# Order of the last output blocks and the last LayerNorm of a two-layer decoder trunk

## The chip, the core and the metric

One core of a Trainium2 chip runs the whole program. The metric is device time in microseconds (us) from the start to the end of one execution; before the change the median of three runs is 1009.05 us. The engines named below are the tensor engine (PE, whose weight loads have a row of their own, PEld), the vector engine (DVE), the scalar engine (ACT), GpSimd (POOL) and the sync engine (SP), which here only issues transfers. ACT and POOL issue transfers too.

## The reference, cut to what matters

The trunk has two layers on 256 tokens of width 2048: a Mamba-2 layer and a sliding-window attention layer. Each ends in a residual sum and a LayerNorm. The change touches the very last part: the output projection of the attention layer, the residual sum and the last LayerNorm.

```python
def _layernorm(x, g, b):
    xf = x.astype(jnp.float32)
    mu = jnp.mean(xf, axis=-1, keepdims=True)
    var = jnp.mean(jnp.square(xf - mu), axis=-1, keepdims=True)
    y = (xf - mu) * lax.rsqrt(var + EPS) * g.astype(jnp.float32) + b.astype(jnp.float32)
    return y.astype(x.dtype)
...
    o = o * jax.nn.silu(gate)
    return o @ w_out
...
        x = _layernorm(ALPHA * x + h, ln_g[layer], ln_b[layer])
    return x
```

## The kernel before, in words

**Tiles.** The 256 tokens are two halves, h = 0 and h = 1, of 128 tokens each, one token to a partition. The residual stream is the tile `xr`, 128 partitions x 2 halves x 2048. The 2048 output columns are four blocks nb (c in the norm) of 512.

**Weights.** A unit is 128 x 2048 weights. It comes in two 512 KB transfers into `wr` (line 131, SP's queue) and is split into a rounded part `wh` (ACT, line 140) and the remainder `wl` (DVE, line 141). `next_unit()` hands out the next unit and loads two ahead.

**One output block** is `out_unit` (line 278): for one half and one block, 12 matmuls of 128x128 by 128x512 (lines 284 to 286: high by high, low by high, high by low, for four slices of the contraction) into one of four PSUM buffers `mm`; then DVE adds the sum to `xr` (line 293). After each block `norm_stats` (line 752) takes mean and variance of it on DVE.

**The end** is `out_last` (line 295), called for the last quarter of the contraction, whose four units hold all blocks nb = 0 to 3. Its order before: half 0 block 0, half 1 block 0, then half 0 blocks 1 to 3, then `done2(0)`, then half 1 blocks 1, 2 and 3 (block 3 as two blocks of 256 columns), then `done2(1)`.

**`done2(0)`**, the norm of half 0: `norm_scale` merges the statistics on DVE (line 756) and takes the reciprocal root by Ln and Exp on ACT (lines 758, 759). For each of four blocks: DVE makes t = (xr - mean) * g (line 1094), ACT scales t (line 1097), POOL adds b (line 1098), SP sends the block out (line 1099). This runs beside the matmuls of half 1.

**`done2(1)`**, the norm of half 1: nothing but this is left to do. PE puts b into three PSUM tiles `ax` (identity times b, line 1068; blocks 0 and 1 whole and half of block 2). ACT makes a diagonal `dg` of the scale (line 1069), DVE makes t for all four blocks (line 1074), PE adds `dg` times t (line 1080), ACT copies the sums to `xr` (line 1081) and sends them (line 1082). The other half of block 2 and block 3 are finished on DVE (line 1085) and sent by SP (line 1088).

**Order.** Each engine runs its instructions in the order in which the program was recorded (with some movement by the recording layer, which `keep_in_program_order` forbids for the instruction that it is given); engines wait for each other by semaphores. The buffers `t` (tag `pt`) are four.

Of the kernel before, what the change touches and what calls it, by code (L numbers as in the profile page):

```python
# [8 lines left out]
F32 = mybir.dt.float32  # L9
# [3 lines left out]
AF = mybir.ActivationFunctionType  # L13
ALU = mybir.AluOpType
AX = mybir.AxisListType

P = 128
# [48 lines left out]
def trunk(ctx: ExitStack, tc: tile.TileContext, A: dict, out: bass.AP, dbg=None):  # L66
    nc = tc.nc
    PSUM = bass.MemoryType.PSUM

    def pool(name, bufs=1, side=None, space=None, stack=ctx):  # L70
        kw = {"space": space} if space is not None else {}
        return stack.enter_context(
            tc.tile_pool(name=name, bufs=bufs, side=side, reuse_waits="tile", **kw)
        )
# [9 lines left out]
    def nm(s):  # L84
        uid[0] += 1
        return f"{s}_{uid[0]}"

    def mm_tile():
        return mm_ps.tile([P, 512], F32, tag="mm", name=nm("mm"), bufs=4)

    def ax_tile():
        return ax_ps.tile([P, 512], F32, tag="ax", name=nm("ax"), bufs=4)

    cc = cst.tile([P, 896], F32, tag="cc", name="cc")
    ident = cc[:, 0:128]
# [117 lines left out]
    def next_unit():  # L213
        load_next(min(used[0] + 1 + AHEAD, len(srcs)) - len(units))
        used[0] += 1
        return units[used[0] - 1]
# [29 lines left out]
    xr = xp.tile([P, 2 * D + 120], F32, tag="xr", name="xr")[:, : 2 * D].rearrange("p (h d) -> p h d", h=2)  # L246
# [27 lines left out]
    def pinned(m, pin):  # L274
        if pin:
            tc.keep_in_program_order(m)

    def out_unit(aH, aL, h, u, nb, first, rms=None, pin=False, c0=0, c1=512):

        ps = mm_tile()[:, : c1 - c0]  # L280
        hs = slice(h * P, (h + 1) * P)
        for k in range(4):
            ks = slice(k * 512 + c0, k * 512 + c1)
            pinned(nc.tensor.matmul(ps, aH[:, k, hs], u.h[:, ks], start=k == 0, stop=False), pin)  # L284
            pinned(nc.tensor.matmul(ps, aL[:, k, hs], u.h[:, ks], start=False, stop=False), pin)  # L285
            pinned(nc.tensor.matmul(ps, aH[:, k, hs], u.l[:, ks], start=False, stop=k == 3), pin)  # L286
        v = xr[:, h, nb * 512 + c0 : nb * 512 + c1]
        if first:
            nc.vector.scalar_tensor_tensor(v, v, ALPHA, ps, ALU.mult, ALU.add)
        elif rms is not None:  # L290
            nc.vector.scalar_tensor_tensor(v, ps, rms[:, h : h + 1], v, ALU.mult, ALU.add)  # L291
        else:
            nc.vector.tensor_tensor(v, v, ps, ALU.add)

    def out_last(aH, aL, stats, done):

        us = []
        for nb in range(4):
            us.append(next_unit())
            out_unit(aH, aL, 0, us[nb], nb, False)  # L300
            stats(0, nb)
            if nb == 0:
                out_unit(aH, aL, 1, us[nb], nb, False)
                stats(1, nb)
        done(0)
        for nb in range(1, 4):

            n = 256 if nb == 3 else 512
            for c0 in range(0, 512, n):
                out_unit(aH, aL, 1, us[nb], nb, False, None, False, c0, c0 + n)  # L310
                stats(1, nb, c0, c0 + n)
        done(1)

    def narrow(ps, u, k0, k1, pin=False):
        for k in range(k0, k1):
# [387 lines left out]
    for g in range(NG):  # L703
        t = 10 * g
# [44 lines left out]
    x1L = x1s.tile([P, KT, S], F32R, tag="x1L", name="x1L")  # L749

    def norm_stats(st, h, nb, c0=0, c1=512):
        nc.vector.bn_stats(st[:, h, nb + (c0 > 0), :], xr[:, h, nb * 512 + c0 : nb * 512 + c1])

    def norm_scale(lp, st, h, n=4):
        mv = lp.tile([P, 2], F32, tag="mv", name=nm("mv"), bufs=2)
        nc.vector.bn_aggr(mv[:], st[:, h, :n, :])
        rs = lp.tile([P, 1], F32, tag="rs", name=nm("rs"), bufs=2)
        nc.scalar.activation(rs[:], mv[:, 1:2], AF.Ln, bias=eps_t[:])
        nc.scalar.activation(rs[:], rs[:], AF.Exp, scale=-0.5)
        return mv, rs  # L760
# [42 lines left out]
    us = {}  # L803
    yHL, rms = gs[NG - 1].y, gs[NG - 1].rms
    for h, nb in ((0, 0), (1, 0), (0, 1), (0, 2), (0, 3), (1, 1), (1, 2), (1, 3)):
        if h == 0:
            us[nb] = next_unit()
        out_unit(*yHL, h, us[nb], nb, False, rms, True)
        norm_stats(st1, h, nb)
        if nb == 3:  # L810
            center(h)
        for c in {(1, 2): (0, 1), (1, 3): (2, 3)}.get((h, nb), ()):
            turn_x1(0, c, x1p, "x1", 2)
# [4 lines left out]
    bp = pool("bp")  # L818
# [36 lines left out]
    for h in range(2):  # L855
        ps = mm_tile()
# [43 lines left out]
    os_ = {}  # L900
# [153 lines left out]
    gp = pool("gp", side="right")  # L1054
    gb2 = [gp.tile([P, D], F32, tag=f"gb{i}", name=f"gb2_{i}") for i in range(2)]
    nc.gpsimd.dma_start(gb2[0][:], A["lng"][1].partition_broadcast(P))
    nc.gpsimd.dma_start(gb2[1][:], A["lnb"][1].partition_broadcast(P))
    st2 = bp.tile([P, 2, 5, 6], F32, tag="st", name="st2")

    def done2(h):  # L1060
        mv, rs = norm_scale(bp, st2, h, 4 + h)
        if h:

            dg = bp.tile([P, P], F32, tag="dg", name="dg")
            ends = (512, 512, 256, 0)
            pss = [ax_tile()[:, :n] for n in ends[:3]]
            for c, ps in enumerate(pss):
                nc.tensor.matmul(ps, ident, gb2[1][:, c * 512 : c * 512 + ends[c]], start=True, stop=False)
            nc.scalar.activation(dg[:], ident, AF.Copy, scale=rs[:])
            ts = []  # L1070
            for c in range(4):
                sl = slice(c * 512, (c + 1) * 512)
                t = bp.tile([P, 512], F32, tag="pt", name=nm("t"), bufs=4)
                nc.vector.scalar_tensor_tensor(
                    t[:], xr[:, h, sl], mv[:, 0:1], gb2[0][:, sl], ALU.subtract, ALU.mult
                )
                ts.append(t)
                if ends[c]:
                    sl = slice(c * 512, c * 512 + ends[c])
                    nc.tensor.matmul(pss[c], dg[:], t[:, : ends[c]], start=False, stop=True)  # L1080
                    nc.scalar.copy(xr[:, h, sl], pss[c])
                    nc.scalar.dma_start(out[h * P : (h + 1) * P, sl], xr[:, h, sl])
            for c in (3, 2):
                sl = slice(c * 512 + ends[c], (c + 1) * 512)
                nc.vector.scalar_tensor_tensor(
                    xr[:, h, sl], ts[c][:, ends[c] :], rs[:], gb2[1][:, sl], ALU.mult, ALU.add
                )
                nc.sync.dma_start(out[h * P : (h + 1) * P, sl], xr[:, h, sl])
            return
        for c in range(4):  # L1090
            sl = slice(c * 512, (c + 1) * 512)
            v = xr[:, h, sl]
            t = bp.tile([P, 512], F32, tag="pt", name=nm("t"), bufs=4)
            nc.vector.scalar_tensor_tensor(
                t[:], v, mv[:, 0:1], gb2[0][:, sl], ALU.subtract, ALU.mult
            )
            nc.scalar.activation(t[:], t[:], AF.Copy, scale=rs[:])
            nc.gpsimd.tensor_tensor(v, t[:], gb2[1][:, sl], ALU.add)
            nc.sync.dma_start(out[h * P : (h + 1) * P, sl], v)

    if PRE:
        tc.keep_in_program_order(nc.scalar.preload_act_table_set("natural_log_exp_and_others"))
    out_last(*os_[3], lambda *a: norm_stats(st2, *a), done2)


def _layout(inputs):
# [88 lines left out]
```

## Time and profile before

| | us |
|---|---|
| median of three runs | 1009.05 (1008.87 to 1010.24) |
| the profiled execution: its own time | 1009.92 |
| its span, first to last instruction | 1008.0 |
| last matmul of `out_unit` starts | 997.25 |
| last transfer is issued | 1003.65 |

The profile gives times in us from the start of the span. A row of the time-ordered view reads: start, duration, engine, line, operation, what is written from what, shapes, the count of instructions that were merged into the row, and in brackets the idle time of the engine before it and what ended it. A "q" behind an engine (SPq, ACTq) is its sequencer, where transfers are issued. Matmuls are pipelined: a row's duration is longer than the distance to the next one. A float32 matmul of 512 columns shows as two records.

### The profile page before, as it was taken

The page shows a single profiled execution, that of the slowest core. Times are in us where ns is not written, and L with a number is a line of the kernel's source. Part 1 is how long each engine was busy: PE and PEld are TensorE (multiplying, and loading weights), DVE is VectorE, ACT ScalarE, POOL GpSimd, SP SyncE. Part 2 cuts the span into 40 slices and gives each one's busy share as a digit, 9 for nine tenths or more (in the row PEclk, how much of TensorE's full clock was granted, in tenths as well). Part 3 has the DMA queues.
Part 4 walks back from the last instruction along what each step waited for, and adds up shares of the span by engine and source line. Part 5 has one row for each costly group of instructions (what it writes and reads, how often), then busy time and mean ns, then how long its engine had stood idle before and what let it go on. Part 6 is the DMA issues. An engine that isn't in the chain of part 4 may idle for free.

```text
span 1008.0 us, 17712 instructions
## 1 busy us (share of the span) xinstructions
PE 995.8 (99%) x7027; PEld 901.7 (89%) x7027; DVE 770.5 (76%) x1133; ACT 566.6 (56%) x947; POOL 103.5 (10%) x126
## 2 busy tenths in 40 slices
PE   8999999999999999999999999999999999999997
PEld 7999989999998998999999999888988878878975
DVE  5778977877786887686787687898688775775686
ACT  5576856647655654664654664566545543543642
POOL 0000403004003002100300300403000000000002
PEclk9999999999999999999999999999999999999999
DMA  8797576565666766656656556557754545545532
GB/s 316 264 290 251 207 249 195 173 238 164 216 211 187 228 197 201 202 191 201 206 175 224 154 187 221 168 160 246 232 196 140 185 149 180 174 147 178 173 129 84
DMA packets 58386, 198.80 MB, mean 197 GB/s; under 512 B 6496, under 2 KB 11008, under 8 KB 58048
## 3 DMA queue, kind: packets, MB, share of 16 engines
q1 hardware_dynamic: 55216, 188.20, 57.5%
q0 software_dynamic: 2336, 8.69, 2.7%
q8 instruction: 55, 0.90, 0.4%
q10 hardware_dynamic: 752, 0.79, 0.2%
q14 instruction: 27, 0.22, 0.1%
HBM read 195.43 MB, written 2.23 MB: 196 GB/s over the span
## 4 chain that ended last, share of the span: by engine, by line
PE 85%; DVE 6%; ACT 4%; DMA 3%; issue 2%; SPq 0%; ACTq 0%; DVEq 0%
PE mm L220 43%; PE mm L284 8%; PE mm L285 8%; PE mm L286 8%; PE mm L846 3%; PE mm L847 3%; PE mm L848 3%; DVE wl L141 2%; PE ax L564 2%; DMA wr<-in_wa 2%; PE ax L956 1%; PE ax L1014 1%; DVE cv L431 1%; ACT wh L140 1%; ACT e L484 1%
## 5 line engine op out<-in xcount | busy, mean ns | idle before, releaser
L141 DVE TENSOR_TENSOR wl<-wr,wh 128x1024 fp32r<-128x1024 f32 (+2 forms) x342 | 398.5, 1183 | 116.9 <-ACT wh L140 115.5
L140 ACT ACTIVATE wh<-wr 128x1024 fp32r<-128x1024 f32 (+2 forms) x342 | 337.8, 1011 | 218.9 <-PE mm L220 79.2
L220 PE MATMUL mm<-xH,wh 128*128 128x256 f32 x1280 | 356.5, 279 | 0.0
L220 PE MATMUL mm<-xL,wh 128*128 128x256 f32 x1280 | 355.5, 278 | 0.0
L220 PE MATMUL mm<-xH,wl 128*128 128x256 f32 x1280 | 355.2, 278 | 0.0
L220 PEld LDWEIGHTS mm<-xH,wh 128*128 128x128 f32 x1280 | 241.2, 188 | 2.2 <-ACT wh L173 0.7
L220 PEld LDWEIGHTS mm<-xL,wh 128*128 128x128 f32 x1280 | 241.2, 188 | 1.0
L220 PEld LDWEIGHTS mm<-xH,wl 128*128 128x128 f32 x1280 | 241.2, 188 | 0.0
L284 PE MATMUL mm<-wh,yH 128*128 128x512 f32 x256 | 101.5, 396 | 0.3 <-DVE xr L291 0.3
L285 PE MATMUL mm<-wh,yL 128*128 128x512 f32 x256 | 99.8, 390 | 0.0
L286 PE MATMUL mm<-wl,yH 128*128 128x512 f32 x256 | 99.7, 390 | 0.0
L580 POOL TENSOR_TENSOR yz<-yz,z 128x256 f32<-128x256 f32 x32 | 32.7, 1031 | 478.0 <-DVE yz L575 478.0
L431 DVE SCALAR_TENSOR_TENSOR cv<-mm,pc,cv 128x255 f32<-128x255 f32 x144 | 68.8, 478 | 5.3 <-ACT cv L429 4.0
L220 PE MATMUL mm<-x1H,wh 128*128 128x256 f32 x256 | 71.9, 281 | 0.0
L220 PE MATMUL mm<-x1H,wl 128*128 128x256 f32 x256 | 71.0, 277 | 0.0
L220 PE MATMUL mm<-x1L,wh 128*128 128x256 f32 x256 | 71.0, 277 | 0.0
L846 PE MATMUL mm<-wh,x1H 128*128 128x512 f32 x160 | 63.2, 395 | 0.0
L847 PE MATMUL mm<-wh,x1L 128*128 128x512 f32 x160 | 62.5, 391 | 0.2 <-DVE x1L L799 0.2
L848 PE MATMUL mm<-wl,x1H 128*128 128x512 f32 x160 | 62.4, 390 | 0.0
L284 PEld LDWEIGHTS mm<-wh,yH 128*128 128x128 f32 x256 | 48.1, 188 | 11.0 <-DVE z L517 1.0
L291 DVE SCALAR_TENSOR_TENSOR xr<-mm,r,xr 128x512 f32<-128x512 f32 x64 | 47.0, 745 | 13.4 <-PE mm L286 8.8
L286 PEld LDWEIGHTS mm<-wl,yH 128*128 128x128 f32 x256 | 48.1, 188 | 10.2
(192 smaller groups left out, 1331.8 us busy)
## 6 DMA issues: line engine op xcount, KB each, us to landing
wr<-in_wa SPq DMA_DIRECT2D x158, 512.0 KB, 4.9
wr<-in_wo SPq DMA_DIRECT2D x64, 512.0 KB, 4.2
wr<-in_wq SPq DMA_DIRECT2D x32, 512.0 KB, 4.5
wr<-in_wg SPq DMA_DIRECT2D x32, 512.0 KB, 4.7
wr<-in_wb SPq DMA_DIRECT2D x32, 512.0 KB, 4.6
rb<-rscr SPq DMA_DIRECT2D x11, 512.0 KB, 5.0
wr<-in_wkv SPq DMA_DIRECT2D x8, 512.0 KB, 4.5
el<-rscr SPq DMA_DIRECT2D x14, 256.0 KB, 4.7
```

The costliest lines, as they stand in the source:

```text
L140: nc.scalar.activation(h[:, sl], v, AF.Copy)
L141: m = nc.vector.tensor_tensor(l[:, sl], v, h[:, sl].bitcast(F32), ALU.subtract)
L220: m = nc.tensor.matmul(ps, a, b, start=first and i == 0, stop=last and i == 2)
L284: pinned(nc.tensor.matmul(ps, aH[:, k, hs], u.h[:, ks], start=k == 0, stop=False), pin)
L285: pinned(nc.tensor.matmul(ps, aL[:, k, hs], u.h[:, ks], start=False, stop=False), pin)
L286: pinned(nc.tensor.matmul(ps, aH[:, k, hs], u.l[:, ks], start=False, stop=k == 3), pin)
L291: nc.vector.scalar_tensor_tensor(v, ps, rms[:, h : h + 1], v, ALU.mult, ALU.add)
L431: nc.vector.scalar_tensor_tensor(a[:, sft:], ps[:, : S - sft], w(3 - sft), a[:, sft:], ALU.mult, ALU.add)
L580: nc.gpsimd.tensor_tensor(v, v, st.z[i][:], ALU.mult)
L846: pinned(nc.tensor.matmul(ps[:], x1H[:, kk, hs], u.h[:, ks], start=kk == 0, stop=False), pin)
L847: pinned(nc.tensor.matmul(ps[:], x1L[:, kk, hs], u.h[:, ks], start=False, stop=False), pin)
L848: pinned(nc.tensor.matmul(ps[:], x1H[:, kk, hs], u.l[:, ks], start=False, stop=kk == KT - 1), pin)
```

## The change

`out_last` now takes all four blocks of half 0 first, then all four of half 1 (block 3 in two again). The norm of half 0 is in two parts: blocks 0 and 1 are handed to DVE, ACT and POOL right after half 0's statistics, block 2 after half 1's block 0, block 3 after half 1's block 1. For half 1's blocks 0 and 1, DVE makes xg = xr * g as soon as the block is there, without the mean.

The norm of half 1 uses two diagonals for blocks 0 and 1: `dg[0]` holds the scale, `dg[1]` the scale times the negative mean (`nmean`, on DVE). PE sums identity times b, `dg[0]` times xg and `dg[1]` times g. Blocks 3 and 2 are done wholly on DVE, each by two instructions. The transfers out are then issued in the order 3, 0, 2 from SP, and 1 from ACT. Nearly all instructions of this end are pinned to the order written.

```diff
-    def out_last(aH, aL, stats, done):
+    def out_last(aH, aL, stats, first_done, product, last_done):
...
         for nb in range(4):
             us.append(next_unit())
             out_unit(aH, aL, 0, us[nb], nb, False)
             stats(0, nb)
-            if nb == 0:
-                out_unit(aH, aL, 1, us[nb], nb, False)
-                stats(1, nb)
-        done(0)
-        for nb in range(1, 4):
+        rest = first_done()
+        for nb in range(4):
 
             n = 256 if nb == 3 else 512
             for c0 in range(0, 512, n):
                 out_unit(aH, aL, 1, us[nb], nb, False, None, False, c0, c0 + n)
                 stats(1, nb, c0, c0 + n)
-        done(1)
+            if nb < 2:
+                product(nb)
+                rest(2 + nb)
+        last_done()
...
+    xg = gp.tile([P, 2, 512], F32, tag="xg", name="xg")
...
+    def product2(nb):
+        sl = slice(nb * 512, (nb + 1) * 512)
+        ordered(nc.vector.tensor_tensor(xg[:, nb, :], xr[:, 1, sl], gb2[0][:, sl], ALU.mult))
+
+    def first_done2():
+        mv, rs = norm_scale(bp, st2, 0, 4)
+
+        def piece(c):
...
+            ordered(
+                nc.vector.scalar_tensor_tensor(t[:], v, mv[:, 0:1], gb2[0][:, sl], ALU.subtract, ALU.mult)
             )
             nc.scalar.activation(t[:], t[:], AF.Copy, scale=rs[:])
             nc.gpsimd.tensor_tensor(v, t[:], gb2[1][:, sl], ALU.add)
+            nc.sync.dma_start(out[0:P, sl], v)
+
+        piece(0)
+        piece(1)
+        return piece
+
+    def last_done2():
+
+        pss = [ax_tile() for _ in range(2)]
+        for c, ps in enumerate(pss):
+            nc.tensor.matmul(ps, ident, gb2[1][:, c * 512 : c * 512 + 512], start=True, stop=False)
+        mv, rs = norm_scale(bp, st2, 1, 5)
+        nmean = bp.tile([P, 1], F32, tag="nmean", name="nmean")
+        ordered(nc.vector.tensor_scalar(nmean[:], mv[:, 0:1], -1.0, None, ALU.mult))
+        dg = bp.tile([P, 2, P], F32, tag="dg", name="dg")
+        ordered(nc.scalar.activation(dg[:, 0, :], ident, AF.Copy, scale=rs[:]))
+        ordered(nc.scalar.activation(dg[:, 1, :], dg[:, 0, :], AF.Copy, scale=nmean[:]))
+        for c, ps in enumerate(pss):
+            ordered(nc.tensor.matmul(ps, dg[:, 0, :], xg[:, c, :], start=False, stop=False))
+            sl = slice(c * 512, (c + 1) * 512)
+            ordered(nc.tensor.matmul(ps, dg[:, 1, :], gb2[0][:, sl], start=False, stop=True))
+            ordered(nc.scalar.copy(xr[:, 1, sl], ps))
+        for c in (3, 2):
...
+            ordered(nc.vector.scalar_tensor_tensor(
+                t[:], xr[:, 1, sl], mv[:, 0:1], gb2[0][:, sl], ALU.subtract, ALU.mult
+            ))
+            ordered(nc.vector.scalar_tensor_tensor(
+                xr[:, 1, sl], t[:], rs[:], gb2[1][:, sl], ALU.mult, ALU.add
+            ))
+        for c, eng in ((3, nc.sync), (0, nc.sync), (2, nc.sync), (1, nc.scalar)):
+            sl = slice(c * 512, (c + 1) * 512)
+            ordered(eng.dma_start(out[P : 2 * P, sl], xr[:, 1, sl]))
...
-    out_last(*os_[3], lambda *a: norm_stats(st2, *a), done2)
+    out_last(*os_[3], stats2, first_done2, product2, last_done2)
```

More of the change, by code (lines that the diff above doesn't have):

```diff
@@ L751, in norm_stats @@
     def norm_stats(st, h, nb, c0=0, c1=512):
-        nc.vector.bn_stats(st[:, h, nb + (c0 > 0), :], xr[:, h, nb * 512 + c0 : nb * 512 + c1])
+        return nc.vector.bn_stats(st[:, h, nb + (c0 > 0), :], xr[:, h, nb * 512 + c0 : nb * 512 + c1])
     def norm_scale(lp, st, h, n=4):
@@ L1058, in trunk @@
     st2 = bp.tile([P, 2, 5, 6], F32, tag="st", name="st2")
[L1060 to L1090, printed above, removed]
@@ L1091, in done2, with stats2 @@
+    xg = gp.tile([P, 2, 512], F32, tag="xg", name="xg")
+    ordered = tc.keep_in_program_order
+    def stats2(h, nb, c0=0, c1=512):
+        ordered(norm_stats(st2, h, nb, c0, c1))
+    def product2(nb):
[4 more added lines that the diff above has]
+        def piece(c):
             sl = slice(c * 512, (c + 1) * 512)
-            v = xr[:, h, sl]
+            v = xr[:, 0, sl]
@@ L1093, in done2 @@
             t = bp.tile([P, 512], F32, tag="pt", name=nm("t"), bufs=4)
-            nc.vector.scalar_tensor_tensor(
-                t[:], v, mv[:, 0:1], gb2[0][:, sl], ALU.subtract, ALU.mult
+            ordered(
+                nc.vector.scalar_tensor_tensor(t[:], v, mv[:, 0:1], gb2[0][:, sl], ALU.subtract, ALU.mult)
             )
@@ L1098, in done2 @@
             nc.gpsimd.tensor_tensor(v, t[:], gb2[1][:, sl], ALU.add)
-            nc.sync.dma_start(out[h * P : (h + 1) * P, sl], v)
+            nc.sync.dma_start(out[0:P, sl], v)
[19 more added lines that the diff above has]
+            sl = slice(c * 512, (c + 1) * 512)
+            t = bp.tile([P, 512], F32, tag="pt", name=nm("t"), bufs=4)
+            ordered(nc.vector.scalar_tensor_tensor(
[5 more added lines that the diff above has]
+        for c, eng in ((3, nc.sync), (0, nc.sync), (2, nc.sync), (1, nc.scalar)):
+            sl = slice(c * 512, (c + 1) * 512)
+            ordered(eng.dma_start(out[P : 2 * P, sl], xr[:, 1, sl]))
     if PRE:
         tc.keep_in_program_order(nc.scalar.preload_act_table_set("natural_log_exp_and_others"))
-    out_last(*os_[3], lambda *a: norm_stats(st2, *a), done2)
+    out_last(*os_[3], stats2, first_done2, product2, last_done2)
 def _layout(inputs):
```

## The prediction

> **What bounds the kernel now.** I read the page first, then the chain of waits, then the time-ordered view of the last 35 us, engine by engine.
>
> ```profile
> span 1008.0 us, 17712 instructions
> ...
> PE 995.8 (99%) x7027; PEld 901.7 (89%) x7027; DVE 770.5 (76%) x1133; ACT 566.6 (56%) x947; POOL 103.5 (10%) x126
> ...
> PE 85%; DVE 6%; ACT 4%; DMA 3%; issue 2%; SPq 0%; ACTq 0%; DVEq 0%
> ```
>
> PE bounds the whole, and the change takes no matmul of the projection away. What can move is the tail, in which the chain leaves PE. Here is DVE in it:
>
> ```profile
> 976.58 2.36 DVE L141 TENSOR_TENSOR wl<-wr,wh 128x1024 fp32r<-128x1024 f32 x2 [0.23 <-ACT wh L140]
> ...
> 986.54 0.69 DVE L293 TENSOR_TENSOR xr<-xr,mm 128x512 f32<-128x512 f32 x1 [1.30 <-PE mm L286]
> 987.26 0.69 DVE L752 BATCH_NORM_STATS2 st<-xr 128x6 f32<-128x512 f32 x1
> 989.26 0.69 DVE L293 TENSOR_TENSOR xr<-xr,mm 128x512 f32<-128x512 f32 x1 [1.30 <-PE mm L286]
> 989.99 0.69 DVE L752 BATCH_NORM_STATS2 st<-xr 128x6 f32<-128x512 f32 x1
> 990.71 0.26 DVE L756 BATCH_NORM_AGGREGATE mv<-st 128x2 f32<-128x24 f32 x1
> 991.01 3.78 DVE L1094 SCALAR_TENSOR_TENSOR t<-xr,mv,gb 128x512 f32<-128x512 f32 x4
> 994.72 0.68 DVE L293 TENSOR_TENSOR xr<-xr,mm 128x512 f32<-128x512 f32 x1
> 995.43 0.69 DVE L752 BATCH_NORM_STATS2 st<-xr 128x6 f32<-128x512 f32 x1
> 996.04 0.67 DVE L293 TENSOR_TENSOR xr<-xr,mm 128x512 f32<-128x512 f32 x1
> ...
> 998.14 0.40 DVE L293 TENSOR_TENSOR xr<-xr,mm 128x256 f32<-128x256 f32 x1
> 998.58 0.43 DVE L752 BATCH_NORM_STATS2 st<-xr 128x6 f32<-128x256 f32 x1
> 999.04 0.29 DVE L756 BATCH_NORM_AGGREGATE mv<-st 128x2 f32<-128x30 f32 x1
> 999.43 2.74 DVE L1074 SCALAR_TENSOR_TENSOR t<-xr,mv,gb 128x512 f32<-128x512 f32 x4
> ```
>
> Up to 989.26 DVE idles 1.30 us before each add: PE sets the pace, one block per 2.72 us. From 991.01 it never idles again: the four subtractions of half 0 put it behind PE, whose last projection matmul starts at 997.25 and ends at 997.53 (next fence), while the last add starts at 998.14. So 0.56 us of the tail (998.14 less 997.58, taking 0.05 from PE's end to the add) is DVE's backlog. I call the end of half 1's aggregate A; here A = 999.33. After A:
>
> ```profile
> 999.36 0.30 ACT rs L758
> ...
> 999.69 0.21 ACT rs L759
> ...
> 999.93 0.41 ACT dg L1069
> ...
> 1000.38 1.14 PE ax L1080 x2
> ...
> 1001.54 0.59 ACT xr L1081
> ...
> 1002.16 0.38 ACTq L1082
> ```
> ```profile
> 997.25 0.28 PE L286 MATMUL mm<-wl,oH 128*128 128x256 f32 x1
> 997.38 2.31 PE L1068 MATMUL ax<-gb,cc 128*128 128x512 f32 x6
> ```
> ```profile
> 998.23 0.19 PEld L1068 LDWEIGHTS ax<-gb,cc 128*128 128x128 f32 x1 [0.24 <-issue]
> 998.66 0.19 PEld L1068 LDWEIGHTS ax<-gb,cc 128*128 128x128 f32 x1 [0.24 <-PE ax L1068]
> ```
> ```profile
> L1082 ACTq DMA_DIRECT2D out<-xr x3: 360/381/415, 1002.2 to 1003.7; - x3
> ...
> DMA to landing us min/median/max: 2.0/2.1/2.7
> ```
>
> A to PE's first diagonal matmul is 1.05 (1000.38 less 999.33). A float32 matmul of 512 columns is two records, 0.43 apart (998.23 to 998.66), so 0.86; the copy starts 1.16 after the first starts (1001.54 less 1000.38): 0.86 and 0.30 of latency. The last transfer is issued at 1003.7, and with the longest landing, 2.7 behind four others, lands at 1006.4; 1.6 more end the span.
>
> **The order of halves.** In the built program PE does the twelve matmuls of every block as before, four blocks of half 0 and then half 1, so its end, 997.53, does not move. Half 0 is complete one block earlier: its last add at 986.54 and not 989.26, aggregate from 987.99 to 988.25. The fourth unit is needed 2.72 earlier, at about 983.6; its remainder was ready at 978.94 (976.58 and 2.36), so this costs nothing while 4.7 us of cover stand. Each later block still finds its PSUM buffer read: DVE is never four blocks late.
>
> **What DVE does before A.** It gains two products xg; the price is that of line 890, a multiplication of two SBUF tensors of the same size: 0.69.
>
> ```profile
> L890 DVE TENSOR_TENSOR xr<-xr,gb x8: 684/686/693, 696.2 to 764.0; 128x512 f32<-128x512 f32 x8
> ```
>
> Whether that fits depends on POOL, which adds b for half 0 at the same time:
>
> ```profile
> 991.86 1.99 ACT L1097 ACTIVATE t<-t,rs 128x512 f32<-128x512 f32 x3 [0.32 <-DVE t L1094]
> ```
> ```profile
> 993.00 1.79 DVE L1094 SCALAR_TENSOR_TENSOR t<-xr,mv,gb 128x512 f32<-128x512 f32 x1
> ```
> ```profile
> 992.67 1.58 POOL L1098 TENSOR_TENSOR xr<-t,gb 128x512 f32<-128x512 f32 x1 [42.78 <-ACT t L1097]
> ...
> 994.20 1.75 POOL L1098 TENSOR_TENSOR xr<-t,gb 128x512 f32<-128x512 f32 x1
> ...
> 995.91 1.29 POOL L1098 TENSOR_TENSOR xr<-t,gb 128x512 f32<-128x512 f32 x1
> ```
> ```profile
> L595 DVE SCALAR_TENSOR_TENSOR yL<-yz,pc,yH x32: 473/831/959, 107.0 to 637.9; 128x256 fp32r<-128x256 f32 x32
> ```
>
> The fourth subtraction takes 1.79 and not 0.75: POOL's first addition ran from 992.67 to 994.25, and the subtraction ends 0.54 after that. The next addition, in turn, takes 1.75 beside that subtraction, against 1.29 alone. The adds of line 293 (one input from PSUM) and the statistics keep 0.68 and 0.69 in the same stretch. I read: an instruction of DVE with two SBUF inputs and a POOL addition exclude each other, in turn. Line 595 shows the same earlier, 473 to 959 ns. A subtraction ending at 994.79 took hold at 994.04, so POOL excludes DVE until 0.21 before its end, 1.06 from its own hold; DVE excludes POOL until about 0.1 before its end. The new order puts four such DVE instructions (two xg, two subtractions) between the adds. Pitches from the rows: 0.67 after an unblocked subtraction, 0.70 from add to statistics, 0.61 from there on; ACT ends t 0.8 before POOL can start.
>
> Half 0's two first subtractions start at 988.29 and 988.96; ACT scales from 989.14 (991.86 less 2.72), POOL adds from 989.95 (992.67 less 2.72). Then:
> - add of block 0 at 989.64, statistics 990.34, xg at 990.95, held to 991.01, done 991.70. POOL's second addition, ready, gets its hold at about 991.58 and excludes until 992.64.
> - subtraction of block 2 waits from 991.63 to 992.64 and ends at 993.39; POOL's third addition starts at 994.30.
> - add of block 1 at 993.32 (PE had it at 991.98), statistics 994.02, xg at 994.63 held to 995.36, done 996.05; subtraction of block 3 at 995.98, free.
> - add of block 2 at 996.66. Before, it came at 996.04, and A 3.29 later; so A = 999.95, later by 0.62.
>
> Bounds: with no exclusion the same list puts the add of block 2 at 994.87, DVE waits for PE's end, and A = 997.58 + (999.33 − 998.14) = 998.77. That is the lower end. The upper end is that each of the three held instructions waits for the whole addition, 1.27 and not 1.06: xg ends at 991.91, the subtraction runs 993.18 to 993.93, POOL's third addition ends at 996.11, xg at 996.80, and A = 1000.70.
>
> [...] The row of 1.79 us has the exclusion, but a hold shorter by 0.21, and the row decides.
>
> **What follows A.** `nmean` is one element per partition; the nearest row is 0.21:
>
> ```profile
> L773 DVE TENSOR_SCALAR nmr<-mv,rs x2: 209/212/216, 662.6 to 675.1; 128x1 f32<-128x1 f32 x2
> ```
>
> It ends at A + 0.26, before the scale (A + 0.57), so it holds only the subtraction behind it, by 0.15 or so. The second diagonal costs ACT another 0.40 and a 0.04 gap, but lies under PE's first matmul, from A + 1.05 to A + 1.91: PE would need it then and has it at A + 1.5. If that cover were gone it would cost 0.45. PE now has four matmuls of 0.86, two to each tile, where it had two and a half. Block 0's copy starts at A + 1.05 + 1.72 + 0.30 = A + 3.07, and is sent by SP at A + 3.7. Block 1's starts at A + 1.05 + 3.44 + 0.30 = A + 4.79, ends at A + 5.38, and its transfer is issued at A + 5.41; before, the last one was issued at A + 4.3. DVE's four instructions (two that read the result just written) end at A + 3.2, and block 2's transfer stands behind block 0's on SP, at A + 4.0: neither is last. The last transfer runs nearly alone: 2.05 and not 2.7. With 1.62 to the end: A + 9.08, against A + 8.64 before. So the new tail costs 0.44: 1.09 of later issue less 0.65 of landing.
>
> **Sum.** 999.95 + 9.08 = 1009.03 of span, 1.05 over 1007.98. The profiled execution took 1009.92, its span and 1.9 around it; that is 0.9 above the median of 1009.05. By the same difference it would take 1010.97, and the median 1010.1.
>
> **The rivals.**
> - *No exclusion on the new instructions* (A = 998.77): 0.13 below before, 1008.9. For it: POOL may come a little later, and 0.33 decide whether xg or POOL's third addition is first. Against: the 1.79 row.
> - *A hold for the whole addition* (A = 1000.70): 1.8 over, 1010.9. For it: spans on POOL are rough. Against: the overlap of 0.21.
> - *PE loses its clock, clearly slower.* Between the matmuls of line 1068 (four records, over at about 999.2) and the first diagonal one at 1001.0 PE idles 1.8 us, before 1.2 (to 1000.38); should the clock be halved there, eight records take 0.86 each and the end comes 3.4 later: 1013.5.
>
> ```profile
> 1003.00:1006.00 3.00, 0.00 (x0) 0.00 (x0) 0.23 (x1) 0.44 (x2) 0.00 (x0) 1.00 0.93 350
> ...
> 1006.60:1008.00 1.40, 0.00 (x0) 0.00 (x0) 0.00 (x0) 0.00 (x0) 0.00 (x0) 0.50 0.01 6
> ```
>
> The third number from the end is the granted clock: PE is idle from 1002.8, and the clock is still full at 1006.0, halved at 1006.6. It decides from an idle time of more than 3.2 us, which even A = 1000.70 (2.6) doesn't reach.
>
> **How the numbers follow.** Forecast 0.60, its own range 1009.4 to 1010.9; no exclusion 0.13; whole hold 0.20; clock 0.07. The three runs of before lie 1.4 apart, so 0.2% (2.0 us) is about what can be told: the bounds are 1007.0 and 1011.1. Faster takes a span below every case here: 0.03. Slower is the clock's 0.07, a third of the whole hold's 0.20 and a tenth of the forecast's 0.60 (scatter takes these over the bound): 0.07 + 0.07 + 0.06 = 0.20; same 0.77. The range reaches from the case without exclusion less 0.4 of scatter to the whole hold and 0.9 of it: 1008.5 to 1011.8.
>
> **What would show it.** In the changed profile: PE without a gap to 997.5; half 0's aggregate near 988.2; xg or the subtraction after it stretched to 1.4 us or more where a POOL addition overlaps; half 1's aggregate ending near 1000.0; ACT's last copy 5.4 and the end 9.1 after it. A stretched xg missing, or the end nearer than 8.6 to A, makes the forecast wrong; so does a granted clock below 1.00 before the last matmul.

## The result and the profile after

| | before | after |
|---|---|---|
| median of 12 runs each, us | 1010.04 (1008.87 to 1010.47) | 1010.98 (1010.40 to 1014.38) |
| ratio after / before | | 1.002, 95% interval 1.0012 to 1.0029 |
| profiled execution: its own time | 1009.92 | 1013.43 |
| its span | 1008.0 | 1011.4 |

The change makes the kernel slower by about 0.2%: small, but the interval leaves 1 out. This ratio lies near that of the means (1011.83 and 1009.83), which four late runs of after (1013.43 to 1014.38) pull up; the medians lie 0.94 apart, 0.09%. The predicted 1010.1 stood 1.05 above the 1009.05 that was then known of before; now both medians stand about 0.9 higher than thought.

The page of the changed kernel, engine by engine and then the shares of its chain of waits:

```profile
PE 998.0 (99%) x7027; PEld 902.5 (89%) x7027; DVE 771.5 (76%) x1134; ACT 566.9 (56%) x947; POOL 103.4 (10%) x126
...
PE 88%; DVE 5%; ACT 3%; DMA 2%; issue 1%; SPq 0%; ACTq 0%; DVEq 0%
```

PE has as many instructions as before (7027) and still 99% of the span. The profiled span grew by 3.4, much more than the tail was to grow. So two questions: is the tail as predicted, and where do the other 2.3 us come from?

The tail first, in the time-ordered view of DVE (start, duration, engine, line, operation, count):

```profile
988.80 0.69 DVE L293 TENSOR_TENSOR xr<-xr,mm 128x512 f32<-128x512 f32 x1 [1.30 <-PE mm L286]
...
990.25 0.26 DVE L756 BATCH_NORM_AGGREGATE mv<-st 128x2 f32<-128x24 f32 x1
990.55 1.42 DVE L1079 SCALAR_TENSOR_TENSOR t<-xr,mv,gb 128x512 f32<-128x512 f32 x2
...
993.21 0.84 DVE L1069 TENSOR_TENSOR xg<-xr,gb 128x512 f32<-128x512 f32 x1
993.97 1.77 DVE L1079 SCALAR_TENSOR_TENSOR t<-xr,mv,gb 128x512 f32<-128x512 f32 x1
...
996.99 1.44 DVE L1069 TENSOR_TENSOR xg<-xr,gb 128x512 f32<-128x512 f32 x1
998.35 0.74 DVE L1079 SCALAR_TENSOR_TENSOR t<-xr,mv,gb 128x512 f32<-128x512 f32 x1
...
1002.01 0.29 DVE L756 BATCH_NORM_AGGREGATE mv<-st 128x2 f32<-128x30 f32 x1
1002.33 0.15 DVE L1096 TENSOR_SCALAR nmean<-mv 128x1 f32<-128x1 f32 x1
```

POOL and PE beside it:

```profile
992.21 1.29 POOL L1082 TENSOR_TENSOR xr<-t,gb 128x512 f32<-128x512 f32 x1 [39.63 <-ACT t L1081]
993.46 1.73 POOL L1082 TENSOR_TENSOR xr<-t,gb 128x512 f32<-128x512 f32 x1
996.58 1.29 POOL L1082 TENSOR_TENSOR xr<-t,gb 128x512 f32<-128x512 f32 x1 [1.39 <-ACT t L1081]
```
```profile
999.51 0.28 PE L286 MATMUL mm<-wl,oH 128*128 128x256 f32 x1
```

The last DVE add before half 0's aggregate starts at 988.80, after 1.30 us of idling: PE sets the pace there, as before. Then the first xg is held for a moment (0.84; free it takes 0.68, below), the subtraction behind it for longer (1.77 where 0.74 is free), and the second xg again (1.44). Each ends 0.55 or 0.56 after a POOL addition: those end at 993.50, 995.19 and 997.87, the three DVE instructions at 994.05, 995.74 and 998.43. PE's last projection matmul ends at 999.79; half 1's aggregate (A in the prediction) ends at 1002.30, 2.50 later, where it was 1.79 later before.

What follows A, on ACT and PE:

```profile
1003.35 1.12 PE L1101 MATMUL ax<-xg,dg 128*128 128x512 f32 x2 [1.83 <-ACT dg L1098]
1006.03 1.02 PE L1103 MATMUL ax<-gb,dg 128*128 128x512 f32 x2
```
```profile
1005.37 0.59 ACT L1104 COPY xr<-ax 128x512 f32<-128x512 f32 x1 [1.64 <-PE ax L1103]
1007.09 0.59 ACT L1104 COPY xr<-ax 128x512 f32<-128x512 f32 x1 [1.13 <-PE ax L1103]
1007.70 0.38 ACTq L1116 DMA_DIRECT2D out<-xr  x1
```

The two copies start 3.07 and 4.79 after A, the last transfer is issued 5.40 after it: the figures of the prediction to 0.01. The end comes 9.12 after A, predicted 9.08.

The other 2.3 us: PE's end itself moved, from 997.53 to 999.79, though its work up to there is the same. By stretches of 3.4 us (columns: the stretch, its length, busy time and count of PE, PEld, DVE, ACT and POOL, granted clock, DMA share, GB/s), after and then before:

```profile
92.20:95.60 3.40, 1.40 (x13) 0.81 (x11) 2.18 (x7) 2.25 (x4) 0.00 (x0) 1.00 0.89 275
95.60:99.00 3.40, 2.94 (x18) 2.09 (x20) 3.40 (x9) 3.24 (x5) 0.00 (x0) 0.50 0.19 77
```
```profile
92.20:95.60 3.40, 2.45 (x25) 1.63 (x25) 2.49 (x7) 3.40 (x5) 0.00 (x0) 1.00 0.74 236
95.60:99.00 3.40, 3.40 (x34) 2.85 (x32) 3.40 (x6) 3.25 (x6) 0.00 (x0) 1.00 0.17 42
```

In this run after, PE was busy for only 1.40 of the 3.40 us before 95.6, and then ran at half clock until 99.0: 18 matmuls where before has 34. The wait that emptied it, in the views of PE's weight loads, after and then before:

```profile
94.61 0.63 PEld L564 LDWEIGHTS ax<-e,xd 128*64 128x64 f32 x8 [2.08 <-DVE xd L546]
```
```profile
93.28 0.63 PEld L564 LDWEIGHTS ax<-e,xd 128*64 128x64 f32 x8 [0.56 <-DVE xd L546]
```

That is the first layer, 900 us away from anything that the change touches. The same matmul of the two runs, counted in order, starts 0.19 earlier in after at 92 us, 1.54 later at 95 and 2.62 later at 97: the wait costs about 1.7 and the half clock 1.1. Some 0.4 is made up later, and 2.26 is left at the end.

The wait itself goes back to a transfer of weights. ACT's rounding of a piece of weights (line 140), released by that transfer, starts 1.33 later in after, and the first xd (line 546) as much later, 94.14 against 92.81; from this rounding to xd it is 5.63 or 5.64 in all ten traces of this document.

```profile
88.50 1.06 ACT L140 ACTIVATE wh<-wr 128x1024 fp32r<-128x1024 f32 x1 [0.41 <-DMA wr<-in_wa]
```
```profile
87.17 1.06 ACT L140 ACTIVATE wh<-wr 128x1024 fp32r<-128x1024 f32 x1 [0.53 <-DMA wr<-in_wa]
```

### The profile page after: what moved, and what is told of

The parts are those of the page before. It is cut to its first block, busy times and chain, and to the rows that moved or that the text cites. A ratio compares the mean times of both kernels' runs of the same rounds, so it can differ in the third digit from the quotient of the medians.

```text
span 1011.4 us, 17715 instructions
## 1 busy us (share of the span) xinstructions
PE 998.0 (99%) x7027; PEld 902.5 (89%) x7027; DVE 771.5 (76%) x1134; ACT 566.9 (56%) x947; POOL 103.4 (10%) x126
## 4 chain that ended last, share of the span: by engine, by line
PE 88%; DVE 5%; ACT 3%; DMA 2%; issue 1%; SPq 0%; ACTq 0%; DVEq 0%
PE mm L220 45%; PE mm L284 8%; PE mm L285 8%; PE mm L286 8%; PE mm L846 3%; PE mm L847 3%; PE mm L848 3%; PE ax L564 2%; DMA wr<-in_wa 2%; DVE wl L141 2%; PE ax L956 1%; PE ax L1014 1%; ACT wh L140 1%; PE ax L996 1%; PE ax L541 1%
```

## The experiments

To keep the two apart, every run below is read by its trace with these figures. E is the end of the last projection matmul (the start of its record and 0.28). A is the end of half 1's aggregate. R is the span's end less E: what the tail costs after PE. In before, A − E = 1.79, end − A = 8.65, R = 10.44; in after 2.50, 9.12 and 11.62. So R rose by 1.18 (predicted 1.05), and E by 2.26 (predicted 0). Theory 1: the change costs R + 1.2, of which 0.7 is the exclusion of DVE and POOL and 0.5 the longer tail after A, and E scatters from run to run whatever the kernel. The rivals: the change brings the clock drop with it; or the late A has another cause than POOL.

**The same kernel once more** (no edit).

> The changed kernel once more, nothing altered. Let R be the time from the end of the last projection matmul (start of its record and 0.28 us) to the end of the span: 10.45 us before, 11.62 us after the change. Theory 1 (the tail costs about 1.1 us and the rest of the first measurement's excess is a stall and a clock drop near 95 us of the span that has nothing to do with the change): R is 11.6 again to within 0.1 whatever the time, undisturbed runs lie at 1010.4 to 1010.8, some runs lie 1.5 to 4 us above, and such runs turn up for the kernel before as well. Rival (the change itself brings the clock drop): about 4 of 10 runs again above 1012, and none of the kernel before.

R was 11.62 again (2.50 and 9.11), to the hundredth, and E 997.67 with the clock full:

```profile
92.20:95.60 3.40, 1.50 (x16) 0.97 (x16) 2.25 (x7) 3.34 (x5) 0.00 (x0) 1.00 0.78 266
95.60:99.00 3.40, 3.40 (x37) 2.76 (x33) 3.40 (x7) 3.24 (x6) 0.00 (x0) 1.00 0.12 41
```

PE has a thin stretch here too (1.50), but no drop follows. Twelve runs had a median of 1010.96 against 1009.71 of 23 runs of before: ratio 1.0008 (means 1010.71 and 1010.00), interval 0.9999 to 1.0017, which just takes 1 in. R's 1.18 is 0.12% of the time, and lies in this interval and at the low end of the first one. The times did not fall as expected: they reach from 1009.22 to 1012.12, four of them below 1010.4, and none has a low mean clock. So runs of one kernel scatter by 2.9 us without losing the clock.

**Before once more** (no edit).

> The kernel of before once more. Theory 1 (what differs between runs of one kernel is laid down before the last projection matmul, and the tail repeats): R is 10.45 to within 0.05, while the last projection matmul may end anywhere from 996.5 to 1000. Rival (the tail varies from run to run by as much as the kernels differ): R is off by 0.3 or more.

R was 10.45, and here it is before that has the drop:

```profile
91.70:95.10 3.40, 1.64 (x17) 0.98 (x17) 2.22 (x7) 3.01 (x5) 0.00 (x0) 1.00 0.88 257
95.10:98.50 3.40, 3.40 (x24) 2.25 (x20) 3.40 (x7) 3.25 (x5) 0.00 (x0) 0.50 0.10 28
```
```profile
93.35 0.63 PEld L564 LDWEIGHTS ax<-e,xd 128*64 128x64 f32 x8 [1.38 <-DVE xd L546]
```

So the drop belongs to both kernels, and the rival that the change brings it falls. By an estimate, half of 3.4 us in a span of 1010, a halved clock for 3.4 us takes about 0.0017 off a run's mean granted clock. Runs with a mean of 0.998 or less: 4 of 12 in the first measurement of after (1013.43 to 1014.38; the other eight have a median of 1010.5 and a mean of 1010.81), none of 12 in the second; of before 3 of 23 beside that, and 2 of 17 in a later round. These counts, 4 of 24 and 5 of 40, do not show that the change makes the drop more frequent, nor do they rule it out.

**The new order with the old norm.** `product2` does nothing, and `last_done2` does for half 1 what `done2(1)` did.

```diff
     def product2(nb):
-        sl = slice(nb * 512, (nb + 1) * 512)
-        ordered(nc.vector.tensor_tensor(xg[:, nb, :], xr[:, 1, sl], gb2[0][:, sl], ALU.mult))
+        pass
...
     def last_done2():
...
-        dg = bp.tile([P, 2, P], F32, tag="dg", name="dg")
...
+        dg = bp.tile([P, P], F32, tag="dg", name="dg")
+        ends = (512, 512, 256, 0)
+        pss = [ax_tile()[:, :n] for n in ends[:3]]
...
```

> New order of blocks, but half 1's norm as before: no xg, one diagonal, subtractions for all four blocks after the statistics. Theory 1 (two xg that exclude POOL's additions make the aggregate late, and two more float32 matmuls make the last copy late): the aggregate ends 1.25 us after the last projection matmul (after the change 2.5, before 1.8), the end is 8.65 after that, R = 9.9, and the time is 0.5 us below before and 1.7 below after. Rival (the new order itself costs, since half 0's norm now runs wholly beside DVE's adds): the aggregate stays at 2.0 or later and R at 10.6 or more.

A − E = 1.25, end − A = 8.65, R = 9.90, the tail as expected. DVE in it:

```profile
990.53 0.84 DVE L1077 SCALAR_TENSOR_TENSOR t<-xr,mv,gb 128x512 f32<-128x512 f32 x1
...
992.89 1.42 DVE L1077 SCALAR_TENSOR_TENSOR t<-xr,mv,gb 128x512 f32<-128x512 f32 x1
...
997.15 0.42 DVE L293 TENSOR_TENSOR xr<-xr,mm 128x256 f32<-128x256 f32 x1 [0.56 <-PE mm L286]
```

POOL still stretches two subtractions (0.84 and 1.42), but without the two xg there is room for it: DVE idles 0.56 before the last add, waiting for PE. Eleven runs of it had a median of 1008.57: ratio to before 0.9986, interval 0.9978 to 0.9995. This half of the change alone is faster than before, and its median is 2.39 below that of after in the same round. But 1.14 below before was 0.5 in the expectation and is 0.54 in R: the other 0.6 is not in the tail, and no run ties it to the order.

**The old order with the new norm.** Half 1's block 0 goes back between half 0's first two blocks, and half 0's four pieces stand together.

```diff
             stats(0, nb)
+            if nb == 0:
+                out_unit(aH, aL, 1, us[nb], nb, False)
+                stats(1, nb)
+                product(nb)
         rest = first_done()
-        for nb in range(4):
+        rest(2)
+        rest(3)
+        for nb in range(1, 4):
...
-                rest(2 + nb)
```

> The order of blocks as before, with the changed norm of half 1 (two diagonals, xg of block 0 right after half 1's block 0, xg of block 1 after half 1's block 1). Half 0's four subtractions then stand together again, and xg of block 1 falls on POOL's third addition. Theory 1 (exclusion, and the new order itself is a gain): that xg takes about 1.6 us and not 0.69, the aggregate ends 3.4 after the last projection matmul (after the change 2.5), the end comes 9.1 after it, R = 12.5. Rival (the order is what costs): the aggregate ends no later than 2.5, R at most 11.6.

A − E = 3.17, R = 12.29, each 0.2 less than expected. The xg of block 1 is held until POOL lets it go (1.71), and what follows it is packed closely: two adds in one row, then the statistics of both. Whether that is the 0.2 is not shown.

```profile
995.09 1.71 DVE L1074 TENSOR_TENSOR xg<-xr,gb 128x512 f32<-128x512 f32 x1
996.72 1.00 DVE L293 TENSOR_TENSOR xr<-xr,mm 128x512 f32<-128x512 f32 x2
997.65 1.01 DVE L757 BATCH_NORM_STATS2 st<-xr 128x6 f32<-128x512 f32 x2
```

With this the two parts of the change stand in a table of R:

| R, us | old norm | new norm | the norm's part |
|---|---|---|---|
| old order | 10.44 | 12.29 | +1.85 |
| new order | 9.90 | 11.62 | +1.72 |
| the order's part | −0.54 | −0.67 | |

**No additions on POOL.** The transfers of half 0 read t; the addition of b in half 0 is left out, and nothing else.

```diff
-            nc.gpsimd.tensor_tensor(v, t[:], gb2[1][:, sl], ALU.add)
-            nc.sync.dma_start(out[0:P, sl], v)
+            nc.sync.dma_start(out[0:P, sl], t[:])
```

> The changed kernel without POOL's additions of b for half 0 (half 0 is sent without b). Theory 1 (exclusion): xg and the subtractions take 0.69 and 0.75 each, the aggregate ends 1.25 us after the last projection matmul and not 2.5, R = 10.4. Rival (the bare work of the two products on DVE delays the aggregate, 1.4 us of it): the aggregate ends 2.2 or later, R at least 11.3.

```profile
989.97 0.68 DVE L1069 TENSOR_TENSOR xg<-xr,gb 128x512 f32<-128x512 f32 x1
990.56 0.75 DVE L1079 SCALAR_TENSOR_TENSOR t<-xr,mv,gb 128x512 f32<-128x512 f32 x1
...
992.55 0.68 DVE L1069 TENSOR_TENSOR xg<-xr,gb 128x512 f32<-128x512 f32 x1
...
996.60 0.42 DVE L293 TENSOR_TENSOR xr<-xr,mm 128x256 f32<-128x256 f32 x1 [0.56 <-PE mm L286]
```

Both xg take 0.68, the subtraction 0.75, DVE waits for PE again, and A − E is 1.25; end − A stays 9.12. So all of A's lateness (2.50 less 1.25) comes from POOL's additions: DVE has room for the xg themselves. The run with the old norm had the same 1.25 with POOL's additions and without the two xg, so it takes both to make A late.

**One diagonal.** The product of `dg[1]` and g is left out, and with it the mean term in half 1's blocks 0 and 1; `dg[1]` is still made.

```diff
-            ordered(nc.tensor.matmul(ps, dg[:, 0, :], xg[:, c, :], start=False, stop=False))
-            sl = slice(c * 512, (c + 1) * 512)
-            ordered(nc.tensor.matmul(ps, dg[:, 1, :], gb2[0][:, sl], start=False, stop=True))
+            ordered(nc.tensor.matmul(ps, dg[:, 0, :], xg[:, c, :], start=False, stop=True))
+            sl = slice(c * 512, (c + 1) * 512)
```

> The changed kernel without the two matmuls of the second diagonal (the term of the mean is left out for blocks 0 and 1 of half 1; ACT still makes the diagonal). Theory 1 (PE's four matmuls set the last copy): the last copy starts 3.07 us after the aggregate's end and not 4.79, and the end is 7.4 to 7.9 after the aggregate's end and not 9.1 (the transfers then queue behind each other). Rival (DVE's four instructions and SP's queue set the end): 8.6 or more.

A − E stays 2.51; the copies start 2.21 and 3.07 after A, where they were 3.07 and 4.79, and end − A is 7.85. Two matmuls of 0.86 less take 1.72 off the last copy, but only 1.27 off the end: the last issue is now 3.69 after A, with the other transfers still on their way, and the last landing 2.48 after that, where it was 2.04. PE's four records after the one diagonal, and ACT's second copy:

```profile
1000.12 1.98 PE L1101 MATMUL ax<-xg,dg 128*128 128x512 f32 x4 [1.84 <-ACT dg L1098]
```
```profile
1002.14 0.58 ACT L1103 COPY xr<-ax 128x512 f32<-128x512 f32 x1 [0.27 <-PE ax L1101]
```

**A leaner tail, twice.** From the old norm in the new order, only the transfers out are changed: in `lean_tail` they are pinned, four of them on SP's queue.

```diff
-                nc.scalar.dma_start(out[P : 2 * P, sl], xr[:, 1, sl])
...
-            nc.sync.dma_start(out[P : 2 * P, sl], xr[:, 1, sl])
+        for eng, c0, c1 in ((nc.sync, 0, 512), (nc.sync, 1536, 2048), (nc.sync, 512, 1024),
+                            (nc.scalar, 1024, 1280), (nc.sync, 1280, 1536)):
+            tc.keep_in_program_order(eng.dma_start(out[P : 2 * P, c0:c1], xr[:, 1, c0:c1]))
```

> New order with the old norm (as in the run old_norm, R = 9.9), with the transfers of blocks 0 and 1 issued by SP and not by ACT between its copies. Theory 1 (ACT's issue of block 0 holds the next copy up by 0.2, and the transfers at the end are limited by what they move, 1.15 MB): block 1's copy starts 3.07 after the aggregate and not 3.25, the last landing comes 0.1 to 0.3 earlier, R = 9.7, and the time is that of old_norm to within what can be told, 0.1% or so below before. Rival (the issue on ACT is what sets the end): the end comes 0.4 or more earlier, R at most 9.5.

A miss: R = 10.04. DVE finished half of block 2 before block 3, not after it, so block 3 came last, 3.9 after A, and held up block 1's transfer, which stands behind it on SP and was ready at 3.66: it was issued at 4.38, the last at 4.78. (What half 1 moves is 128 x 2048 x 4 bytes, 1.05 MB and not 1.15.) Twelve runs had a median of 1009.25, ratio to before 1.0001 (0.9989 to 1.0012). The second version asks for the transfers in the order in which the blocks come:

```diff
-        for eng, c0, c1 in ((nc.sync, 0, 512), (nc.sync, 1536, 2048), (nc.sync, 512, 1024),
-                            (nc.scalar, 1024, 1280), (nc.sync, 1280, 1536)):
+        for eng, c0, c1 in ((nc.sync, 0, 512), (nc.sync, 1280, 1536), (nc.sync, 512, 1024),
+                            (nc.scalar, 1024, 1280), (nc.sync, 1536, 2048)):
```

> lean_tail with SP's queue in the order in which the pieces get ready: block 0, the half of block 2 that DVE finishes first, block 1, block 3 last. Theory (in lean_tail the transfer of block 1 stood on SP behind that of block 3, which DVE finishes last, 3.9 us after the aggregate): block 1 is issued 3.7 after the aggregate and not 4.4, the last landing comes about 6.9 after it (7.5 in lean_tail, 7.03 with two issues on ACT), R = 9.7 to 9.85. Rival (the transfers together set the end, whatever their order): R stays at 9.9 or more.

SP's queue in the two versions (`lean_tail`, then `lean_tail_2`: start of the first issue, time until the end of the last, four transfers):

```profile
1004.05 2.42 SPq L1114 DMA_DIRECT2D out<-xr  x4
```
```profile
1002.57 1.81 SPq L1114 DMA_DIRECT2D out<-xr  x4
```

The four issues take 1.81 instead of 2.42, and R = 9.70: 0.20 less than the new order with the old norm, 0.74 less than before. R came out as expected, but not by the way expected: the last transfer landed 7.17 after A, not 6.9, and later than the 7.03 of the new order with the old norm. What is shorter is the time from there to the end of the span: 1.28 here and 1.29 in `lean_tail`, where SP's transfer lands last, and 1.62 to 1.68 in the other eight traces, where ACT's does. Why, was not tried. The second version was run once (1010.25 beside 1011.57 of before on the same chip, at a mean clock of 0.999 and 0.997), so this gain is read from the trace's tail alone, and not shown as a time.

## Why the prediction was right and where it was not

**Where the time was to go: right.** The tail, point by point (us):

| | predicted | measured |
|---|---|---|
| first xg, held | 0.75 | 0.84 |
| subtraction of block 2, held | 1.76 | 1.77 |
| second xg, held | 1.42 | 1.44 |
| subtraction of block 3, free | 0.75 | 0.74 |
| A − E, change | +0.62 | +0.71 |
| nmean | 0.21 | 0.15 |
| copies after A | 3.07 and 4.79 | 3.07 and 4.79 |
| last issue after A | 5.41 | 5.40 |
| end − A | 9.08 | 9.12 |
| R, change | +1.05 | +1.18 |

Four observations carry this: half 0's aggregate ends 9.28 before E in after and in every run with the new order, 6.56 before; the xg and the subtractions are stretched where POOL's additions overlap and nowhere else; without those additions A − E is 1.25; without the second product the last copy comes 1.72 earlier. The missing 0.09 of A is mostly the first xg, which met POOL's first addition 0.16 longer than free, not 0.06 (0.84 less 0.68). The 0.04 of end − A that is missing lies behind the last landing: the span ends 1.67 after it, where it was 1.62 in before.

**The rival without exclusion** (A − E = 1.24; the run without POOL's additions has 1.25) and the one with **a hold for the whole addition** (A − E = 3.17 by the list that was predicted for it, 1000.70 less 997.53) both fall: 2.50 lies between them. The held instructions, ending 0.68 or 0.74 after they get hold, got it by that reckoning at 993.37, 995.00 and 997.75, which is 0.13, 0.19 and 0.12 before POOL's recorded ends. However long the instruction was held (0.84, 1.77 and 1.44 against 0.68, 0.74 and 0.68 free), it ended 0.55 or 0.56 after POOL's addition. So by POOL's records the hold ends 0.12 to 0.19 before the addition's record does; how the two engines hold each other up, no run shows.

**"PE's end does not move": right for the change, wrong for a run.** No run shows the change moving E: the ten traces have E between 996.56 and 999.98, and both ends of that range are runs with the new order. But the profiled runs of one and the same kernel differ by 2.12 (999.79 and 997.67) and by 1.32 (997.53 and 998.85). So one of the prediction's own signs of being wrong came in the profiled run, a granted clock below 1.00 before the last matmul (0.50 near 97 us), but not by the change.

**The step that failed** is the one headed "How the numbers follow". It said: "The three runs of before lie 1.4 apart, so 0.2% (2.0 us) is about what can be told", and put the forecast, +1.05, among the cases of no change. Twelve runs a side told more: the interval, 1.0012 to 1.0029, is 0.0017 wide and leaves 1 out. The spread of single runs is not the uncertainty of twelve runs together, and a forecast of +1.05 was a forecast of slower, with its chance to be told as the open question. The four runs with a low clock are about half of the 0.2%: without them the mean of after is 1010.81, 0.98 above that of before, which is the size of the forecast. The second measurement's interval just takes 1 in, so that the changed kernel is slower at all rests on the first one and on R. The same step took the base from three runs whose median, 1009.05, twelve runs then put at 1010.04. And its case of a lost clock had one place, the tail, and one condition, more than 3.2 us of idling, read off a single fall, the one at the end of before; the clock was lost instead near 95 us, in runs of both kernels, where a wait before one weight load was 2.08 us (after) and 1.38 us (before once more). That case needed a row of its own: a run 2 to 4 us up, in some runs of any version. That the medians' 0.94 lies so near the forecast 1.05 is partly luck: the median of the eight other runs of after is 1010.54, only 0.50 above before's. What the scatter of E adds or takes on either side is not known run by run, since E can be read only in the profiled ones. What the prediction says of the tail is borne out by R, 1.18, which repeats to 0.01, and not by that nearness.

**What stays open.** The first xd near 93 us is as late as the transfer of weights that lands at 87.1 in before and 88.4 in after; why that transfer lands at different times in different runs was not tried. Nor was half 0's addition of b on another engine than POOL with its result kept whole.

## What to carry to other kernels

Split a change into its parts before judging it: here the order gained 0.54 to 0.67 and the norm cost 1.72 to 1.85, and only their sum was measured. Work moved to an engine "that has time" is priced by what it meets there: two products of 0.68 on DVE cost 1.25 because POOL was adding at that moment, and a product moved to PE, 0.86 per 512 columns, stood on the path that ends last. And compare a forecast of 0.1% with the interval of the measurement, and tails by a figure such as R, counted from the last event that the change cannot touch.

## What the runs showed of the hardware

PE's clock was halved without PE ever being idle for 3.4 us: PE was busy 1.40 of the 3.40 us before 95.6 in after, with 2.08 as the wait before one weight load, and 1.64 of the 3.40 before 95.1 in the second run of before, with 1.38 as that wait; the granted clock was then 0.50 for 3.4 us each time (95.6 to 99.0, 95.1 to 98.5). The second run of after had 1.50 of 3.40 in the stretch from 92.2 and kept its clock (1.00 from 95.6 to 99.0). So the busy time of one such stretch does not tell by itself which run loses the clock.

The clock also falls after the last matmul: in before at 1006.55, 3.76 after that matmul's record ends, in after at 1010.37, 3.32 after. What follows is an estimate from the times of the falls. In after the two lie 914.77 apart, which is 268 times 3.4133, and the half clock between them lasted 3.413. If the falls of one run always lie a whole number of such steps apart, the fall at the end of a run gives the stretches of 3.41 us to look at in it. PE's busy time in the thinnest of them near 93 us was 1.41 (after), followed by half clock, but 1.75 (`lean_tail_2`), 1.90 (after once more) and 2.46 (before), all at full clock afterwards. In the other two traces with a fall near 95 us, the 3.40 us ahead of it have 1.02 (`lean_tail`, 92.2 to 95.6; clock 0.50 from 95.6 to 99.0) and the 1.64 of before once more. The thin stretch of after once more falls into two (`lean_tail_2`, then after once more):

```profile
91.81:95.22 3.41, 1.75 (x16) 1.16 (x15) 2.19 (x6) 2.45 (x4) 0.00 (x0) 1.00 0.90 275
95.22:98.63 3.41, 3.14 (x31) 2.36 (x32) 3.41 (x8) 3.25 (x5) 0.00 (x0) 1.00 0.14 56
```
```profile
89.64:93.05 3.41, 1.90 (x17) 1.70 (x15) 2.83 (x7) 1.03 (x3) 0.00 (x0) 1.00 0.97 318
93.05:96.46 3.41, 2.35 (x26) 1.50 (x26) 2.77 (x9) 3.25 (x6) 0.00 (x0) 1.00 0.58 203
```

So in these six traces, with the stretches laid so, up to 1.64 was followed by half clock, and 1.75 or more was not. No run was made to place a line between the two, or to test that the falls keep to this step; what makes the clock fall is not shown.
